# Second attention: values of eight heads per token block by three fp32r products of 512 columns from split latent rows and value weights

## The chip, the cores and the metric

The kernel runs on one core of one Trainium2 chip. The metric is the device time of one execution in microseconds (us), lower is better. The engines are named as in the profile: PE is TensorE, PEld its weight loads, DVE VectorE, ACT ScalarE, POOL GpSimd, SP SyncE, whose queue issues most of the loads.

## The reference

The program is two layers of a decoder trunk over 512 tokens of width 1024. Layer 0 mixes tokens by stick-breaking attention, layer 1 by a sparse attention over a latent of 128 values per token; each layer ends in a gated MLP with a short convolution. The change is in layer 1's attention, which is, cut to what matters:

```python
def dsa_attention(h, w_in, q_gain, k_gain, w_uv, w_out, rel_bias):
    q, lat, qi, ki, wi = jnp.split(h @ w_in, [o1, o2, o3, o4], axis=-1)
    q = rms_norm(q.reshape(B, S, 16, 128), q_gain)
    k = rms_norm(lat, k_gain)
    vals = lat
    def block(qb, t):                       # 128 queries at a time
        ...                                 # sel: the 128 keys picked by the indexer
        logits = jnp.einsum('bqhd,bqkd->bqhk', qb, k[bidx, sel]) * scale + bias
        p = jax.nn.softmax(jnp.where(valid, logits, NEG), axis=-1)
        return jnp.einsum('bqhk,bqkd->bqhd', p, vals[bidx, sel])
    o_lat = ...                             # (1, 512, 16, 128)
    o = jnp.einsum('bshl,hlv->bshv', o_lat, w_uv)   # w_uv: (16, 128, 64)
    return o.reshape(B, S, 1024) @ w_out
```

Inputs and results are float32. The kernel uses that the last two steps can be swapped: it first makes per-head values lat x w_uv[h] (512 tokens x 64) and then weights these.

## The kernel before

Tokens are in four blocks of 128. The attention of layer 1 loops over the 16 heads (index h in the code). While the weights of head h are transposed and used, the logits of head n = h + 1 are made. For each head n and each query block j, `logits(n, j)` is three fp32r products (high x high, low x high, high x low) into a PSUM bank z; `softmax(n, j)` is one custom instruction on DVE that adds the masked bias and takes the row maximum (line 1933); `expo(n, j)` is the exponential on ACT (line 2220). `transposed(h, i)` turns the weights of head h on PE in three groups i = 0, 1, 2 (line 2230), the first copied out by ACT (line 2235), the other two by DVE (line 2237). The bias of head h + 2 is prepared by ACT or POOL and masked by POOL (lines 2198, 2200, 2201).

Each engine works its queue in order, and the queue's order is the order in which the code issues the work. Between these steps `fill(n)` puts n steps of other work into PE's queue, three fp32r products each (lines 694 to 696): first the projections of the last q heads (pt_q), then the output projection (pt_o). `follow(engine)` issues what such a step leaves behind on ACT or DVE: the splitting of q (lines 1839, 1840, 1846), of weights (line 644 on ACT and 653 on POOL), and, after the last q head, the sums of squares of the last four q heads: `group_sum(3)`, four fp32 products "ssg" into the bank x (line 1863), copied out by ACT (line 1869).

PSUM has three banks mm, two z, two tr and one x. The bank x is used by the values "pv" and by ssg of the last q group.

Values are made for a pair of heads at a time. `pair_values(h)` is called in every odd iteration for the pair (h - 1, h), between the last logits of the next head and the third group of transposes (in the last iteration after the first group). It is four fp32 products, one for each block of 128 tokens: the latent `latf` is the stationary operand, 128 columns of the value weights `uvc` (two heads) move, and ACT copies the bank to SBUF. `weighted(h)` follows in the next iteration: for each block of keys and each of the two heads one fp32 product with 64 columns of values as the stationary operand (line 2261). Its output is scaled and split into the operands of the output projection (`pair_hi`, `pair_lo`: lines 2296, 2304, 2308).

A "split" of an fp32 tile is a copy on ACT that rounds to fp32r (the high part) and a subtraction on DVE (the low part). `LATE_STEPS` lists how many filler steps stand at each of the three places of an iteration.

Of the kernel before, what the change touches and what calls it, by code (L numbers as in the profile page):

```python
# [9 lines left out]
F32 = mybir.dt.float32  # L10
F32R = mybir.dt.float32r
BF = mybir.dt.bfloat16
AF = mybir.ActivationFunctionType
# [6 lines left out]
S = 512  # L20
P = 128
KT = D // P
QT = S // P
# [550 lines left out]
def kernel_body(ctx, tc, xT, wst, cst, smalls, crow, ccol, relb, outT):  # L574
    nc = tc.nc
    act, dve, pe, pool = nc.scalar, nc.vector, nc.tensor, nc.gpsimd
# [6 lines left out]
    npool = ctx.enter_context(tc.tile_pool(name="npool", bufs=1))  # L583
# [4 lines left out]
    def ptile(shape, name, tag):  # L588
        return banks.tile(shape, F32, name=name, tag=tag, bufs=nbanks[tag])
# [81 lines left out]
    def chunk(key, ahead=AHEAD):  # L671
        if ahead or key not in ready:
            prefetch(order.index(key) + ahead)
        return ready.pop(key)
# [1135 lines left out]
    def dsa_layer(l, first, man):  # L1810
        with ExitStack() as st:
            pp = st.enter_context(tc.tile_pool(name="dsa", bufs=1))
            hs = hcur["h"]
            latf = pp.tile([P, S], F32, name="latf")
# [13 lines left out]
            def project_steps(ps, ck):  # L1828
                whi, wlo = ck
                for k in range(KT):  # L1830
                    w = slice(k * P, (k + 1) * P)
                    mm3(ps, whi[:, w], wlo[:, w], hs[k][0], hs[k][1], k == 0, k == KT - 1)
                    yield
# [59 lines left out]
            def q_newton(h0, h1):  # L1893

                c = slice(h0 * QT, h1 * QT)
                dve.tensor_mul(irq[:, c], rq[:, c], rq[:, c])
                dve.scalar_tensor_tensor(irq[:, c], msq[:, c], EPS, irq[:, c], op0=OP.add, op1=OP.mult)
                dve.scalar_tensor_tensor(rq[:, c], irq[:, c], 3.0, rq[:, c], op0=OP.subtract, op1=OP.mult)
                dve.tensor_scalar(rq[:, c], rq[:, c], -0.5 * P ** -0.5, None, op0=OP.mult)
                dve.reciprocal(irq[:, c], rq[:, c])  # L1900
                act.activation(irq[:, c], irq[:, c], AF.Copy, scale=-1.0)
# [7 lines left out]
            def load_bias(h, th=None):  # L1909
                ths[h] = ap.tile([P, S], F32, name="th", bufs=2) if th is None else th  # L1910
                ov = relb[h:h + 1, 0:1]
                nc.sync.dma_start(ths[h], bass.AP(tensor=ov.tensor, offset=ov.offset, ap=[[1, P], [1, S]]))
# [25 lines left out]
            with ExitStack() as si:  # L1938
# [136 lines left out]
                for h in range(2, EARLY_Q):  # L2075
                    pt = ptile([P, S], "pt_q", "mm")
                    g = project_steps(pt, chunk(("dq", h), 0))
# [40 lines left out]
            with ExitStack() as sa:  # L2118
                ap = sa.enter_context(tc.tile_pool(name="att_d", bufs=2))
                O = []  # L2120
                uvc = [npool.tile([P, S], F32, name="uvc", tag="sqt", bufs=2) for i in range(2)]
# [43 lines left out]
                def fill(n):  # L2165
                    for _ in range(n):
                        next(filler, None)
# [41 lines left out]
                def logits(h, j):  # L2209
                    z = heads[h][3][j] = ptile([P, S], "z", "z")  # L2210
                    logits_into(z, h, j)
# [12 lines left out]
                def transposed(h, pi, by_act):  # L2224
                    tr = ptile([P, S], "tr", "tr")
                    w = TRW[pi]
                    for i, c0 in TRP[pi]:
                        for j in range(i, QT):
                            c = c0 + (j - i) * P
                            pe.transpose(tr[:, c:c + P], Ls[h, j][:, i * P:(i + 1) * P], ident)  # L2230
                    if pi == 0:
                        trs[h] = ap.tile([P, LW], F32, name="pT", bufs=2)
                    t = trs[h][:, TRO[pi]:TRO[pi] + w]
                    if by_act:
                        act.activation(t, tr[:, :w], AF.Copy)
                    else:
                        dve.tensor_copy(t, tr[:, :w])

                vals = {}

                def pair_values(h):

                    pv = ptile([P, S], "pv", "x")
                    for k in range(QT):
                        pe.matmul(pv[:, k * P:(k + 1) * P], lhsT=latf[:, k * P:(k + 1) * P],
                                  rhs=uvc[h // 8][:, h % 8 * 64:h % 8 * 64 + P], start=True, stop=True)
                    vals[h] = npool.tile([P, S], F32, name="vals", tag="u", bufs=3)
                    act.activation(vals[h], pv, AF.Copy)

                def weighted(h):  # L2250

                    av = pair["av"] = ptile([P, S], "av", "mm")
                    ts = [trs.pop(h + e) for e in range(2)]
                    vs = vals.pop(h)
                    for pi in range(3):
                        for i, c0 in TRP[pi]:
                            n = S - i * P
                            c = TRO[pi] + c0
                            for e in range(2):
                                hc = i * P + 64 * e  # L2260
                                pe.matmul(av[64 * e:64 * e + 64, i * P:], lhsT=vs[:, hc:hc + 64],
                                          rhs=ts[e][:, c:c + n], start=i == 0, stop=pi == 2)

                def pair_sums(rv):
# [61 lines left out]
                masked_bias(1, 3)  # L2326
                load_bias(3)
                rvb = None

                def sums(h):  # L2330

                    dve.reciprocal(heads[h][2][:, h % 2], heads[h][1])
                    if h % 2 and h < HEADS - 1:
                        pair_spread(heads[h][2])
                    return pair_sums(heads[h][2]) if h == HEADS - 1 else None

                for h in range(HEADS):
                    n = h + 1
                    more = n < HEADS
                    values = h % 2 == 0 and h > 0  # L2340
                    if more:
                        begin(n)
                        for j in range(2):
                            logits(n, j)
                        softmax(n, 0)
                        expo(n, 0)
                    if values:
                        weighted(h - 2)
                    fill(LATE_STEPS[h][0])
                    transposed(h, 0, True)  # L2350
                    if more:
                        softmax(n, 1)
                        expo(n, 1)
                        sums(h)
                    else:
                        rvb = sums(h)
                        pair_values(h - 1)
                    follow(dve)
                    if h == 3:
                        q_newton(8, EARLY_Q)  # L2360
                    if h == HEADS - 2:
                        late_dots(2)
                    if not more:
                        late_dots(1)
                    if h + 2 < HEADS:
                        masked_bias(h + 2, 0)
                    fill(LATE_STEPS[h][1])
                    if h == 10:
                        follow(dve, 1)
                    if more:  # L2370
                        logits(n, 2)
                        softmax(n, 2)
                        expo(n, 2)
                    transposed(h, 1, False)
                    if "row" in pair:
                        pair_rows()
                    if h + 2 < HEADS:
                        masked_bias(h + 2, 1)
                    if h == 10:
                        follow(dve)  # L2380
                    if more:
                        logits(n, 3)
                        softmax(n, 3)
                        expo(n, 3)
                    if h % 2 and more:
                        pair_values(h - 1)
                    transposed(h, 2, False)
                    if h + 2 < HEADS:
                        for j in range(2, QT):
                            masked_bias(h + 2, j)  # L2390
                    if n + 3 < HEADS:
                        load_bias(n + 3)
                    if h == 1:
                        q_seed(8, EARLY_Q)
                    if values:
                        pair_hi()
                    elif h > 1:
                        pair_lo()
                    fill(LATE_STEPS[h][2])
                    follow(act)  # L2400
                    if h == HEADS - 4:
                        load_dots(3)
                        bias_job(2, "col")
                    if h == 7:
                        follow(dve)
                    if not more:
                        pair_scale(rvb)
# [139 lines left out]
```

## Time and profile before

| | |
|---|---|
| median of 3 runs | 1213.65 us (1213.58 to 1214.35) |
| profiled execution | 1213.79 us, span of its instructions 1212.0 us |
| instructions | 18325 |
| products of the values (pv) | 64 records at line 2245, from 734.4 to 833.9 us |
| granted TensorE clock | 1.00 |

The timeline gives, for each instruction or run of equal ones, start and duration in us from the span's start, engine, line, operation, output<-inputs by the program's names, shape and count; in brackets stand the idle time of the engine before it and what ended it. Matmuls are pipelined: their durations overlap, so their pace is read from their starts. An fp32 product shows as two records. The table by stretches gives length, then busy time and count for PE, PEld, DVE, ACT and POOL, then the granted clock, the DMA share and GB/s.

### The profile page before, as it was taken

How to read it: one execution, taken by the hardware profiler on the slowest of the kernel's cores; microseconds unless marked ns; L12 is line 12 of the kernel's file. 1: busy time of each engine (PE TensorE's matmuls, PEld its weight loads, DVE VectorE, ACT ScalarE, POOL GpSimd, SP SyncE). 2: the span in 40 equal slices, each digit the busy share in tenths (PEclk: the TensorE clock that was granted, in tenths of full speed). 3: DMA queues.
4: the chain of work that ended last, by engine and by line, in shares of the span. 5: the costliest groups of instructions: out<-in, count | busy, mean ns of one | idle time of the engine just before them, and what ended most of it. 6: DMA issues, size and time to landing. Idle time of an engine off the chain costs nothing.

```text
span 1212.0 us, 18325 instructions
## 1 busy us (share of the span) xinstructions
PE 1205.1 (99%) x6532; PEld 1008.3 (83%) x6532; DVE 1032.0 (85%) x1800; ACT 799.8 (66%) x1366; POOL 242.8 (20%) x268
## 2 busy tenths in 40 slices
PE   9999999999999999999999999999999999999998
PEld 6878788788898998998888777777888888888887
DVE  5899888998989989999788995668989898889883
ACT  5588786478666676765657357774786677677660
POOL 0001100001111111211000457884012122112110
PEclk9999999999999999999999999999999999999999
DMA  9668887529889898897520252245499888788662
GB/s 376 236 193 228 231 248 241 202 82 229 192 209 276 230 251 226 221 288 169 189 71 18 71 139 55 88 135 169 132 235 215 224 191 204 183 182 191 153 149 87
DMA packets 79923, 224.50 MB, mean 185 GB/s; under 512 B 16588, under 2 KB 17356, under 8 KB 79832
## 3 DMA queue, kind: packets, MB, share of 16 engines
q1 hardware_dynamic: 59616, 168.77, 42.4%
q0 software_dynamic: 20192, 54.54, 25.3%
q8 instruction: 51, 0.84, 0.3%
q14 instruction: 40, 0.33, 0.1%
q10 hardware_dynamic: 24, 0.02, 0.0%
HBM read 212.23 MB, written 2.16 MB: 177 GB/s over the span
## 4 chain that ended last, share of the span: by engine, by line
PE 97%; DMA 1%; DVE 1%; ACT 1%; issue 0%; SPq 0%; DVEq 0%; ACTq 0%
PE pt_d L1737 16%; PE pt_a L1649 8%; PE pt_u L1618 6%; PE pt_a L1645 6%; PE pt_d L1649 4%; PE pt_u L1622 3%; PE pt_d L1645 3%; PE pt_q L694 2%; PE pt_l L694 2%; PE pt_q L696 2%; PE pt_l L696 2%; PE pt_q L695 2%; PE pt_l L695 2%; PE pt_b L1649 2%; PE pt_qk L694 2%; PE pt_fv L1099 2%
## 5 line engine op out<-in xcount | busy, mean ns | idle before, releaser
L1737 PE MATMUL pt_d<-actlo,dnhi 128*128 128x512 f32 x288 | 112.7, 391 | 0.0
L1737 PE MATMUL pt_d<-acthi,dnhi 128*128 128x512 f32 x288 | 112.7, 391 | 0.0
L1527 ACT ACTIVATE whi<-raw 128x1024 fp32r<-128x1024 f32 x72 | 75.8, 1054 | 29.1 <-PE pt_a L1649 13.2
L644 ACT ACTIVATE whi<-raw 128x1024 fp32r<-128x1024 f32 x80 | 84.2, 1052 | 3.8 <-issue 1.1
L1618 PE MATMUL pt_u<-hh,whi 128*128 128x512 f32 x320 | 75.8, 389 | 0.0
L1737 PE MATMUL pt_d<-acthi,dnlo 128*128 128x512 f32 x288 | 73.5, 390 | 0.0
L662 POOL DMA_DIRECT2D wlo<-wst x23 | 19.9, 866 | 267.3 <-DVE hh L806 115.1
L1618 PEld LDWEIGHTS pt_u<-hh,whi 128*128 128x128 f32 x320 | 60.0, 188 | 12.5
L1539 POOL DMA_DIRECT2D wlo<-wst x37 | 32.0, 865 | 168.5 <-ACT wlo L1535 69.8
L1737 PEld LDWEIGHTS pt_d<-actlo,dnhi 128*128 128x128 f32 x288 | 54.2, 188 | 10.2
L1737 PEld LDWEIGHTS pt_d<-acthi,dnhi 128*128 128x128 f32 x288 | 54.2, 188 | 10.1
L1737 PEld LDWEIGHTS pt_d<-acthi,dnlo 128*128 128x128 f32 x288 | 53.1, 188 | 10.3
L653 POOL TENSOR_TENSOR wlo<-raw,whi 128x1024 fp32r<-128x1024 f32 x18 | 44.2, 2457 | 85.6 <-PE pt_q L695 45.8
L1645 PE MATMUL pt_a<-hh,whi 128*128 128x512 f32 x228 | 61.3, 390 | 0.0
L722 DVE SCALAR_TENSOR_TENSOR raw<-raw,cond 128x1024 f32<-128x1024 f32 x46 | 57.3, 1273 | 1.4 <-ACT cond L1167 1.3
L1649 PE MATMUL pt_a<-hh,wlo 128*128 128x256 f32 x360 | 57.4, 282 | 0.0
L1649 PEld LDWEIGHTS pt_a<-hh,wlo 128*128 128x128 f32 x360 | 53.1, 190 | 4.5
L1346 DVE TENSOR_TENSOR_SCAN mz<-mz,diag 128x128 f32<-128x128 f32 (+1 forms) x64 | 52.5, 820 | 5.2 <-ACT mz L1341 4.9
L1933 DVE CUSTOM_DVE_ANT_0 L<-z,L,cols 128x128 f32<-128x128 f32 (+3 forms) x60 | 32.3, 546 | 28.8 <-PE tr L2230 20.7
L1550 POOL DMA_DIRECT2D whi<-wst x30 | 26.0, 866 | 133.0 <-ACT whi L1547 82.8
L694 PE MATMUL pt_q<-hh,whi 128*128 128x512 f32 x128 | 51.8, 405 | 0.0
L722 DVE SCALAR_TENSOR_TENSOR ada<-ada,cond 128x1024 f32<-128x1024 f32 x41 | 50.0, 1219 | 2.0 <-DMA ada<-wst 2.0
(408 smaller groups left out, 3806.8 us busy)
## 6 DMA issues: line engine op xcount, KB each, us to landing
raw<-wst SPq DMA_DIRECT2D x215, 512.0 KB, 5.1
wlo<-wst POOLq DMA_DIRECT2D x60, 512.0 KB, 8.0
ada<-wst SPq DMA_DIRECT2D x45, 512.0 KB, 5.5
raw<-wst SPq DMA_DIRECT2D x48, 384.0 KB, 4.9
whi<-wst POOLq DMA_DIRECT2D x30, 256.0 KB, 5.7
dnlo<-wst POOLq DMA_DIRECT2D x16, 384.0 KB, 7.0
x<-xt POOLq DMA_DIRECT2D x18, 256.0 KB, 5.3
th<-relb SPq DMA_DIRECT2D x16, 256.0 KB, 3.7
```

The source lines that it names most:

```text
L644: act.activation(hi[:, :n], raw[:, :n], AF.Copy)
L653: engine.tensor_sub(lo[:, :w], raw[:, :w], hi[:, :w].bitcast(F32))
L694: pe.matmul(out, lhsT=whi, rhs=ahi, start=start, stop=False)
L695: pe.matmul(out, lhsT=wlo, rhs=ahi, start=False, stop=False)
L696: pe.matmul(out, lhsT=whi, rhs=alo, start=False, stop=stop)
L722: dve.scalar_tensor_tensor(raw, raw, 1.0, cond, op0=OP.mult, op1=OP.mult, accum_out=dst)
L1346: dve.tensor_tensor_scan(rev, rev, diag[:, S - ns:][:, ::-1], 0.0, OP.mult, OP.max)
L1527: act.activation(W[j, i][0], R[j, i], AF.Copy)
L1618: pe.matmul(pt[j, i], lhsT=W[j, i][0][:, k * P:(k + 1) * P], rhs=hs[k][n], start=k + n == 0, stop=False)
L1645: pe.matmul(pt[j, bank, "both"], lhsT=w[:, c0 + k * P:c0 + (k + 1) * P], rhs=a[2], start=new and k == 0, stop=False, skip_group_check=True)
L1649: pe.matmul(out, lhsT=w[:, c0 + k * P:c0 + (k + 1) * P], rhs=a[n], start=new and k + n == 0, stop=part == 1 and k == 3 and what in ("a2", ...
L1737: pe.matmul(pt["dn", i], lhsT=dn[i][part][:, k * P:(k + 1) * P], rhs=A[j0 + k][n], start=part + k + n == 0, stop=part == 1 and k == j1 - j ...
```

## The change

The values are no longer made for two heads and all four blocks, but for eight heads (512 columns) and one block. The latent and the value weights are split into high and low fp32r parts, `lath`, `latl` and, for each group g of eight heads, `uvh`, `uvl`. One call of `group_values(g, k)` makes the values of block k for group g by three fp32r products of 512 columns into the bank x, which ACT copies out. The eight calls stand in four iterations, two for each group: `value_at` maps (head, place) to (group, block). The places are 0: after the first group of transposes, 1: after the second, 2: between the last logits and the third group. The latent and the weights of group 0 are split ahead of the loop, those of group 1 in iteration 6. `weighted` takes its 64 columns from `vals[h // 8, i]`. Of a group's four blocks three lie in the buffers "u", which held head 0's weights, and the fourth in that of its `uvc`.

```diff
-                def pair_values(h):
+                value_at = {(0, 2): (0, 0), (1, 0): (0, 1), (1, 1): (0, 2), (1, 2): (0, 3),
+                            (8, 0): (1, 0), (8, 2): (1, 1), (9, 0): (1, 2), (9, 2): (1, 3)}
+
+                def spread_values(h, at):
+                    if (h, at) in value_at:
+                        group_values(*value_at[h, at])
+
+                lath = ap.tile([P, S], F32R, name="lath", bufs=1)
+                parts = {"lat": (lath, npool.tile([P, S], F32R, name="latl", tag="ln"))}
+
+                def split_lat():
+                    act.activation(lath, latf, AF.Copy)
+                    dve.tensor_sub(parts["lat"][1], latf, lath.bitcast(F32))
+
+                def split_uv(g):
+                    parts[g] = [ap.tile([P, S], F32R, name="uv" + n, bufs=1) for n in "hl"]
+                    act.activation(parts[g][0], uvc[g], AF.Copy)
+                    dve.tensor_sub(parts[g][1], uvc[g], parts[g][0].bitcast(F32))
+
+                def group_values(g, k):
 
                     pv = ptile([P, S], "pv", "x")
-                    for k in range(QT):
-                        pe.matmul(pv[:, k * P:(k + 1) * P], lhsT=latf[:, k * P:(k + 1) * P],
-                                  rhs=uvc[h // 8][:, h % 8 * 64:h % 8 * 64 + P], start=True, stop=True)
-                    vals[h] = npool.tile([P, S], F32, name="vals", tag="u", bufs=3)
-                    act.activation(vals[h], pv, AF.Copy)
+                    (lh, ll), (uh, ul) = parts["lat"], parts[g]
+                    c = slice(k * P, (k + 1) * P)
+                    pe.matmul(pv, lhsT=lh[:, c], rhs=uh, start=True, stop=False)
+                    pe.matmul(pv, lhsT=lh[:, c], rhs=ul, start=False, stop=False)
+                    pe.matmul(pv, lhsT=ll[:, c], rhs=uh, start=False, stop=True)
+                    tag, bufs = ("u", 3) if k < 3 else ("sqt", 2)
+                    vals[g, k] = npool.tile([P, S], F32, name="vals", tag=tag, bufs=bufs)
+                    act.activation(vals[g, k], pv, AF.Copy)
...
+                split_lat()
+                split_uv(0)
...
                     transposed(h, 0, True)
+                    spread_values(h, 0)
...
-                        pair_values(h - 1)
                     follow(dve)
                     if h == 3:
                         q_newton(8, EARLY_Q)
+                    if h == 6:
+                        split_uv(1)
...
                     transposed(h, 1, False)
+                    spread_values(h, 1)
...
-                    if h % 2 and more:
-                        pair_values(h - 1)
+                    spread_values(h, 2)
                     transposed(h, 2, False)
```

Three places in the engines' queues matter. The first is DVE's queue at the start of head 1's logits (iteration 0). `L` are the masked biases, `th` the bias rows, "ISA" is the maximum of line 1933 and the read of its result; numbers behind a name tell buffers apart. Before:

```order
L1846 TENSOR_TENSOR ql<-pt_q,qh 128x512
L2196 TENSOR_SCALAR L_7379<-th_7230,cols 128x512
L1933 ISA L_7341,nm<-z,L_7341,cols 128x128
L1933 ISA nm 128x1
L1933 ISA L_7363,nm<-z,L_7363,cols 128x256
```

and now:

```order
L1846 TENSOR_TENSOR ql<-pt_q,qh 128x512
L2196 TENSOR_SCALAR L_7381<-th_7230,cols 128x512
L2252 TENSOR_TENSOR latl<-latf,lath 128x512
L2257 TENSOR_TENSOR uvl<-uvc,uvh 128x512
L1933 ISA L_7343,nm<-z,L_7343,cols 128x128
L1933 ISA nm 128x1
L1933 ISA L_7365,nm<-z,L_7365,cols 128x256
```

Two subtractions stand ahead of the first maximum of head 1. In the same way one subtraction stands in iteration 6 between the reciprocal and the maximum of head 7's third block (three of the rows around it):

```order
L2354 RECIPROCAL rv<-sum 128x4
L2257 TENSOR_TENSOR uvl<-uvc,uvh 128x512
L1933 ISA L_7907,nm<-z,L_7907,cols 128x384
L1933 ISA nm 128x1
L2237 COPY pT<-tr 128x512
```

It needs the high part, which ACT makes behind the exponential of head 7's second block. The third place is around the sums of squares of the last q group, at the end of iteration 8. ACT's queue before, from the last exponential of head 9 (`ohi` is the output's split, `whi` that of a weight):

```order
L2220 ACTIVATE L_8061,sum<-L_8061,nm 128x512
L2200 ACTIVATE L_8142<-th,cols 128x384
L2200 ACTIVATE L_8145<-th,cols 128x512
L2304 ACTIVATE ohi<-bo 128x512
L644 ACTIVATE whi<-raw 128x1024
L1869 ACTIVATE sums<-ssg 128x512
L2220 ACTIVATE L_8110,sum<-L_8110,nm 128x128
L2235 ACTIVATE pT<-tr 128x512
L2220 ACTIVATE L_8129,sum<-L_8129,nm 128x256
```

and now:

```order
L2220 ACTIVATE L_8069,sum<-L_8069,nm 128x512
L2269 ACTIVATE vals<-pv 128x512
L2200 ACTIVATE L_8162<-th,cols 128x384
L2200 ACTIVATE L_8165<-th,cols 128x512
L2324 ACTIVATE ohi<-bo 128x512
L644 ACTIVATE whi<-raw 128x1024
L1869 ACTIVATE sums<-ssg 128x512
L2220 ACTIVATE L_8124,sum<-L_8124,nm 128x128
L2235 ACTIVATE pT<-tr 128x512
L2269 ACTIVATE vals<-pv 128x512
```

The copy of ssg out of the bank x now stands between two copies of values out of the same bank. PE's queue at that place, now:

```order
L2264 MATMUL pv<-uvh,lath 128x512
L2265 MATMUL pv<-uvl,lath 128x512
L2266 MATMUL pv<-uvh,latl 128x512
L2230 MATMUL tr<-cons,L_7991 128x128
L2230 MATMUL tr<-cons,L_7994 128x128
L694 MATMUL pt_o<-ohi,whi 128x512
L695 MATMUL pt_o<-ohi,wlo 128x512
L696 MATMUL pt_o<-olo,whi 128x512
L1863 MATMUL ssg<-q2l,ones_r 32x512 x4
L1921 MATMUL z<-kph,qh 128x128
L1922 MATMUL z<-kph,ql 128x128
L1923 MATMUL z<-kpl,qh 128x128
```

Before, the three pv rows at its head were not there; after the rows shown come the second logits of head 10, the first transposes of head 9, and then, now, the values of block (9, 0), where before the filler products stood at once. In the prediction a group product is named by its (head, place).

More of the change, by code (lines that the diff above doesn't have):

```diff
@@ L2253, in weighted @@
                     ts = [trs.pop(h + e) for e in range(2)]
-                    vs = vals.pop(h)
                     for pi in range(3):
@@ L2259, in weighted @@
                             for e in range(2):
-                                hc = i * P + 64 * e
-                                pe.matmul(av[64 * e:64 * e + 64, i * P:], lhsT=vs[:, hc:hc + 64],
+                                hc = (h % 8 + e) * 64
+                                pe.matmul(av[64 * e:64 * e + 64, i * P:], lhsT=vals[h // 8, i][:, hc:hc + 64],
                                           rhs=ts[e][:, c:c + n], start=i == 0, stop=pi == 2)
```

## The prediction

> **What bounds the kernel now.** I read the busy shares first, then the chain that ended last, then one stage in the timeline: the second attention, from the first logits of head 1 to the first product after it.
>
> ```profile
> PE 1205.1 (99%) x6532; PEld 1008.3 (83%) x6532; DVE 1032.0 (85%) x1800; ACT 799.8 (66%) x1366; POOL 242.8 (20%) x268
> ...
> PE 97%; DMA 1%; DVE 1%; ACT 1%; issue 0%; SPq 0%; DVEq 0%; ACTq 0%
> ```
> ```profile
> 724.06:842.00 117.94, 116.75 (x724) 92.37 (x723) 80.67 (x218) 83.03 (x207) 86.20 (x95) 1.00 0.38 109
> ```
>
> TensorE (PE) is busy for 99% of the span and carries 97% of the chain. In this stage it is busy for 116.75 of 117.94 us at a granted clock of 1.00, while the vector engine (DVE) has 80.67 us of work and the scalar engine (ACT) 83.03. So a product taken from TensorE is time won, and a wait put into TensorE's queue is time lost: nothing behind it can pass. What follows is a count of both.
>
> **The products.** Below, z(n,j) are the logits of head n, query block j; tr(h,i) the i-th group of transposes of head h.
>
> ```profile
> 734.12 0.39 PE L1923 MATMUL z<-kpl,qh 128*128 128x512 f32 x1
> 734.35 1.05 PE L2245 MATMUL pv<-uvc,latf 128*128 128x128 f32 x8
> 735.24 0.27 PE L2230 MATMUL tr<-cons,L 128*128 128x128 f32 x1
> ...
> 743.24 0.40 PE L1923 MATMUL z<-kpl,qh 128*128 128x512 f32 x1
> 743.48 0.38 PE L2230 MATMUL tr<-cons,L 128*128 128x128 f32 x2
> ```
> ```profile
> L2245 PE MATMUL pv<-uvc,latf x64: 270/275/275, 734.4 to 833.9; 128*128 128x128 f32 x64
> ```
>
> Durations of matmuls overlap, so starts are read. A pair's four fp32 products (eight records, 64 in all for eight pairs) hold TensorE from 734.35 to 735.24, 0.89 us; in the even head at 743.24 the transposes follow the logits after 0.24 at once. Removed: 8 x 0.89 = 7.12 us. An fp32r product of 512 columns takes 0.23, start to start (734.12 to 734.35). Added: 8 groups of three, 24 x 0.23 = 5.52. Net: 1.60 us less. No more changes between fp32 and fp32r arise than before, since the new products stand beside logits, fillers and transposes as the old did. The evacuations stay eight of the same shape on ACT.
>
> **A gain that doesn't all arrive: head 3.** Six of the eight pairs now find their values ready long before; only weighted(0) and weighted(8) still follow a group closely. One wait for values is in the trace:
>
> ```profile
> 751.36 0.74 DVE L1933 CUSTOM_DVE_ANT_0 L<-z,L,cols 128x512 f32<-128x512 f32 x1
> 752.16 0.38 PE L1921 MATMUL z<-kph,qh 128*128 128x256 f32 x1
> 752.50 0.28 PE L1923 MATMUL z<-kpl,qh 128*128 128x256 f32 x1
> 753.49 0.65 PE L2261 MATMUL av<-pT,vals 128*64 128x512 f32 x2 [0.71 <-ACT vals L2248]
> ```
>
> The wait of 0.71 goes, and 0.89 of product ahead of it too. But z(5,1) at 752.16 starts 0.06 after DVE's maximum of z(4,3) ends (751.36 + 0.74 = 752.10): with TensorE earlier, that maximum is what is late next, and DVE's queue there doesn't depend on the product removed. The weighted product then starts 0.21 after 752.50 at the earliest (0.28 less overlap), 752.71 instead of 753.49. So 0.78 is won at this pair, not 0.89: +0.11 against the sum above. The other odd heads I take at the full 0.89.
>
> **The splits at head 0.** ACT gets two copies and DVE two subtractions ahead of the first maximum of head 1. Their operands are there: latf since the indexer, uvc loaded during the last q projections.
>
> ```profile
> 725.11 0.19 ACT L2220 ACTIVATION_READ_ACCUMULATOR Lu<-Lu,cols 128x1 f32 x1
> 725.30 0.77 DVE L2196 TENSOR_SCALAR L<-th,cols 128x512 f32<-128x512 f32 x1
> 725.99 0.34 DVE L1933 CUSTOM_DVE_ANT_0 L<-z,L,cols 128x128 f32<-128x128 f32 x1
> 726.15 1.16 POOL L2201 TENSOR_TENSOR L<-L,maskb 128x512 f32<-128x512 f32 x1 [0.36 <-DVE L L2196]
> 726.91 0.33 PE L1921 MATMUL z<-kph,qh 128*128 128x384 f32 x1
> ```
> ```profile
> 788.85 0.62 ACT L2304 ACTIVATE ohi<-bo 128x512 fp32r<-128x512 f32 x1
> ```
> ```profile
> 778.56 0.93 POOL L2198 TENSOR_SCALAR L<-th,cols 128x256 f32<-128x256 f32 x1
> 779.10 0.68 DVE L2308 TENSOR_TENSOR olo<-bo,ohi 128x512 fp32r<-128x512 f32 x1
> ...
> 825.24 1.47 DVE L722 SCALAR_TENSOR_TENSOR raw<-raw,cond 128x1024 f32<-128x1024 f32 x1
> 825.58 3.39 POOL L653 TENSOR_TENSOR wlo<-raw,whi 128x1024 fp32r<-128x1024 f32 x1
> 826.64 3.40 DVE L722 SCALAR_TENSOR_TENSOR raw<-raw,cond 128x1024 f32<-128x1024 f32 x1
> ```
>
> The nearest rows to a split are those of the attention's output: 0.62 on ACT, 0.68 on DVE. ACT is free at 725.21 to 725.30, so lath is there by 725.92 and DVE can start latl at 726.00. GpSimd (POOL) has its mask addition L2201 ready at 726.15. At 825.24 such a case stands in the trace: DVE starts, POOL starts 0.34 later and takes 3.39, and DVE's next instruction, of the same kind, then takes 3.40 and ends after POOL: the two take turns whole. I read head 0 the same way: latl 726.00 to 726.68, POOL to 727.84, uvl to 728.52, and only then the maximum of z(1,0), 2.53 late. z(1,2) wants that bank, so it starts at 728.52 + 0.34 + 0.06 = 728.92, not 726.91: TensorE waits 2.01. Bounds: without turns both subtractions are done at 726.00 + 2 x 0.68 = 727.36, and 727.36 + 0.40 - 726.91 = 0.85; if POOL also goes first with its next instruction (0.61, the row at 772.67 below), 2.6. Against the turns speaks the row at 779.10: 0.68 beside a POOL instruction. I keep them, because POOL's instruction here (L2201, a tensor_tensor) is of the kind at 825.58, not of that at 778.56.
>
> The Trainium skill (SBUF — State Buffer, Who interferes with whom) says that a DVE instruction with two SBUF inputs contends with a GpSimd instruction that reads SBUF, and that whichever issues first holds the shared port for the whole instruction. The pair at 825.58 and 826.64 agrees, the pair at 778.56 and 779.10 does not show it; by the rule the sum is my forecast, without it that of the second rival.
>
> **Head 1.** The only bank for values (x) must be emptied between one block and the next, and its evacuation stands behind an exponential on ACT.
>
> ```profile
> 733.53 0.62 DVE L1933 CUSTOM_DVE_ANT_0 L<-z,L,cols 128x384 f32<-128x384 f32 x1 [0.23 <-PE tr L2230]
> 734.19 0.62 ACT L2220 ACTIVATE L<-L,nm 128x384 f32<-128x384 f32 x1 [0.26 <-DVE nm L1933]
> 734.71 0.19 ACT L2220 ACTIVATION_READ_ACCUMULATOR L<-L,nm 128x1 f32 x1
> ...
> 779.27 0.58 ACT L2248 ACTIVATE vals<-pv 128x512 f32<-128x512 f32 x1
> ```
>
> Beside head 0's wait, which moves all engines alike, z(2,2) and with it this chain is two groups later (1.38): the row at 734.71 comes at 736.09, the values of (1,1) are emptied from 736.19 to 736.77. TensorE, three groups later (2.07), wants (1,2) at 734.35 + 2.07 = 736.42 and gets the bank at 736.83: a wait of 0.41. Weighted(0) stands behind two filler steps and the first logits of head 3, so its values are in time.
>
> **The split at head 6.** uvh follows the second exponential on ACT; uvl stands on DVE ahead of the maximum of z(7,2).
>
> ```profile
> 770.30 2.40 POOL L653 TENSOR_TENSOR wlo<-raw,whi 128x1024 fp32r<-128x1024 f32 x1
> 771.67 0.19 ACT L2220 ACTIVATION_READ_ACCUMULATOR L<-L,nm 128x1 f32 x1
> 772.11 0.62 DVE L1933 CUSTOM_DVE_ANT_0 L<-z,L,cols 128x384 f32<-128x384 f32 x1 [3.59 <-PE tr L2230]
> 772.67 0.61 POOL L2198 TENSOR_SCALAR L<-th,cols 128x128 f32<-128x128 f32 x1
> 774.04 0.72 ACT L2220 ACTIVATE L<-L,nm 128x512 f32<-128x512 f32 x1 [0.56 <-DVE nm L1933]
> 774.55 0.49 PE L2230 MATMUL tr<-cons,L 128*128 128x128 f32 x3
> ```
>
> DVE idles for 3.59 us before this maximum, but uvh is finished only at 771.77 + 0.62 = 772.39, so that idle time can't be used. POOL holds until 772.70, uvl runs to 773.38, and the maximum is 1.27 late. So is the exponential at 774.04, which ends (774.76) just as TensorE's fourth transpose of head 7 wants it: no slack, 1.27 of wait. Bounds: 1.02 without turns; 1.9 if POOL's next instruction (772.67, 0.61) goes first.
>
> **Heads 8 and 9.** The sums of squares of the last four q heads (ssg) use the same bank x, between blocks (8,2) and (9,0).
>
> ```profile
> 786.92 1.07 PE L1863 MATMUL ssg<-q2l,ones_r 128*32 128x512 f32 x8
> 787.01 0.72 ACT L2220 ACTIVATE L<-L,nm 128x512 f32<-128x512 f32 x1 [0.56 <-DVE nm L1933]
> 787.73 1.21 ACT L2200 ACTIVATE L<-th,cols 128x384 f32<-128x384 f32 x2
> ...
> 789.06 0.48 PE L694 MATMUL pt_o<-ohi,whi 128*128 128x512 f32 x1
> 789.37 1.04 ACT L644 ACTIVATE whi<-raw 128x1024 fp32r<-128x1024 f32 x1
> 790.32 0.57 ACT L1869 ACTIVATE sums<-ssg 128x512 f32<-128x512 f32 x1
> ```
>
> Block (8,0) makes everything 0.69 later; on ACT the evacuation of (8,2) starts where L2200 did, 787.73 + 0.69 = 788.42, and ends at 789.00. TensorE, two groups later, reaches ssg at 788.30 and waits to 789.06: 0.76. On ACT, L2200 twice, ohi, L644 and the evacuation of ssg take 790.32 + 0.57 - 787.73 = 3.16, so x is free at 792.16. TensorE wants (9,0) where pt_o stood, 789.06 + 1.38 + 0.76 = 791.20, and gets the bank at 792.22: 1.02.
>
> **The sum.** -1.60 + 0.11 + 2.01 + 0.41 + 1.27 + 0.76 + 1.02 = +3.98 us. The profiled execution took 1213.79 us around a span of 1212.0; its own new time would be 1217.8. The median of the runs is 0.14 lower, 1213.65, so the forecast is 1217.6. TensorE carries the chain to the end, so the delay goes through. No DMA is added or moved on any queue.
>
> **Rivals.**
> - The bank is free in time. ACT is idle for 30% of the stage; if its queue ran ahead at heads 1, 8 and 9, 0.41 + 0.76 + 1.02 = 2.19 falls away: 1215.4, not slower by what can be told (0.2%, 2.4 us, is about what a measurement tells from no change). It decides once more than 1.6 of the 2.19 is hidden. Against it: from 787.01 to 790.89 ACT's rows follow each other without a gap.
> - DVE and POOL don't take turns: 2.01 becomes 0.85 and 1.27 becomes 1.02, 1.41 less: 1216.2.
> - POOL goes first twice: 0.6 more at each split: 1218.8.
> - Only the products count, the waits hide: -1.5, 1212.2. For it speaks that DVE and ACT have a third of the stage free; against it, that each place above is in-order and named.
>
> **Numbers.** Forecast 0.52 (own range 1216.6 to 1218.6), bank in time 0.12, no turns 0.18, POOL twice 0.08, products alone 0.10. Slower: the forecast, the fourth case and 0.11 of the third, 0.71. Faster: 0.06, the part of the last case in which the wait for values at head 3 and others like it are won in full too. Same: the rest, 0.23. The range 1214.6 to 1219.6 reaches from the first two rivals together with a little slack to POOL twice and late values at weighted(0) or weighted(8).
>
> **What would show it.** In the trace after: pv as 24 rows at 0.23 steps; z of block 2 of head 1 waiting some 2 us for DVE; ssg and the next pv waiting for ACT 0.8 and 1.0; a late fourth transpose at head 7; uvl longer than 0.68. If those waits are missing, I am wrong towards 1212; if pv steps at more than 0.23, towards more.

## The result, and the profile after

The changed kernel takes 1220.69 us (median of 6 runs, 1220.47 to 1221.36), the kernel before 1213.64 (6 runs beside them): 1.0056 times as long, interval 1.0046 to 1.0067. The forecast was 1217.6, its range ended at 1219.6. Slower was right; of 7.05 us the sum held 3.98.

The page of the changed kernel, its busy times and its chain, then the table by stretches for the same stage, from the first logits of head 1 to the first product after the attention:

```profile
PE 1206.5 (99%) x6492; PEld 1006.3 (83%) x6492; DVE 1036.2 (85%) x1803; ACT 801.0 (66%) x1369; POOL 243.8 (20%) x268
...
PE 88%; DVE 6%; ACT 3%; DMA 1%; issue 1%; POOL 0%; SPq 0%; DVEq 0%; ACTq 0%
```
```profile
724.06:849.00 124.94, 118.37 (x685) 89.63 (x684) 85.05 (x222) 84.71 (x210) 87.40 (x95) 1.00 0.36 103
```

The stage is 7.00 us longer (124.94 for 117.94), which is the whole difference. TensorE is idle in it for 6.57 us instead of 1.19, and the chain runs through DVE for 6% of the span instead of 1%. TensorE's waits in this stage (what waits, for what; us in total, times, longest):

```profile
PE z L1921 <- DVE nm L1933: 3.3, 4, 1.5
PE av L2281 <- DVE pT L2237: 1.1, 1, 1.1
PE ssg L1863 <- ACT vals L2269: 0.7, 1, 0.7
PE pv L2264 <- ACT sums L1869: 0.7, 1, 0.7
PE tr L2230 <- DVE pT L2237: 0.3, 1, 0.3
PE pv L2264 <- ACT vals L2269: 0.2, 1, 0.2
PE tr L2230 <- ACT pT L2235: 0.2, 1, 0.2
```

The first, third, fourth and sixth row are waits of the sum. The second, fifth and seventh are not in it. To size them I laid TensorE's starts in both profiled executions side by side and read by how much each instruction is later than before. This difference is -0.06 just ahead of the first wait, +4.50 at the first filler product behind the first transposes of head 15 (833.96 before, 838.46 now), and +6.80 at the last of head 15's weighted products (838.61 before, 845.41 now). So the loop up to that filler costs 4.56, where the sum had 3.98, and the last few microseconds cost 2.30, where the sum had nothing.

These are the rows of that end, before, in order of time on all engines:

```profile
834.24 0.60 ACT L2248 ACTIVATE vals<-pv 128x512 f32<-128x512 f32 x1
834.74 1.05 ACT L644 ACTIVATE whi<-raw 128x1024 fp32r<-128x1024 f32 x1
...
835.83 0.17 DVE L726 TENSOR_TENSOR mod<-mod,sm 128x8 f32<-128x8 f32 x1
835.87 2.38 POOL L653 TENSOR_TENSOR wlo<-raw,whi 128x1024 fp32r<-128x1024 f32 x1 [6.90 <-ACT whi L644]
835.92 1.01 DVE L2237 COPY pT<-tr 128x512 f32<-128x512 f32 x2
...
836.61 2.37 PE L2261 MATMUL av<-pT,vals 128*64 128x512 f32 x16
```

And now:

```profile
839.84 1.05 ACT L644 ACTIVATE whi<-raw 128x1024 fp32r<-128x1024 f32 x1
840.97 2.63 POOL L653 TENSOR_TENSOR wlo<-raw,whi 128x1024 fp32r<-128x1024 f32 x1 [6.40 <-ACT whi L644]
841.43 2.19 DVE L726 TENSOR_TENSOR mod<-mod,sm 128x8 f32<-128x8 f32 x1
841.49 1.72 PE L2281 MATMUL av<-pT,vals 128*64 128x512 f32 x6
843.55 1.01 DVE L2237 COPY pT<-tr 128x512 f32<-128x512 f32 x2
844.28 1.51 PE L2281 MATMUL av<-pT,vals 128*64 128x384 f32 x10 [1.07 <-DVE pT L2237]
```

Line 726 adds 8 columns; it took 0.17 before. Before, it started 0.04 ahead of GpSimd's subtraction of line 653; now it starts 0.46 behind it and takes 2.19, until GpSimd is done (840.97 + 2.63 = 843.60). The copies of the transposed weights stand behind it in DVE's queue, and the weighted products wait for them. GpSimd starts when ACT's line 644 has made `whi`; before, the evacuation of the last pair's values stood ahead of line 644 on ACT, and the change has taken it away there.

Three theories follow, one for each part of the 7 us. T1: the end of the loop costs about 1.9 because GpSimd now goes ahead of line 726. T2: bank x with one user behind the other costs about 1.7 at heads 8 and 9 (0.75 and 0.91). T3: the subtractions of the splits in DVE's queue cost 1.65 at head 0 and 1.27 at head 6. The expectations below have 1.68 and 1.26 for T3, and 1.03 for the second wait of T2, which there includes that the first product behind the wait lasts longer. Against each theory stands that something else is late there anyway.

### The profile page after: what moved, and what is told of

The parts are those of the page before. It is cut to its first block, busy times and chain, and to the rows that moved or that the text cites. A ratio compares the mean times of both kernels' runs of the same rounds, so it can differ in the third digit from the quotient of the medians.

```text
span 1219.0 us, 18252 instructions
## 1 busy us (share of the span) xinstructions
PE 1206.5 (99%) x6492; PEld 1006.3 (83%) x6492; DVE 1036.2 (85%) x1803; ACT 801.0 (66%) x1369; POOL 243.8 (20%) x268
## 4 chain that ended last, share of the span: by engine, by line
PE 88%; DVE 6%; ACT 3%; DMA 1%; issue 1%; POOL 0%; SPq 0%; DVEq 0%; ACTq 0%
PE pt_d L1737 16%; PE pt_a L1649 8%; PE pt_u L1618 6%; PE pt_a L1645 6%; PE pt_d L1649 4%; PE pt_u L1622 3%; PE pt_d L1645 3%; PE pt_l L694 2%; PE pt_l L696 2%; PE pt_l L695 2%; PE pt_b L1649 2%; PE pt_fv L1099 2%; PE pt_first L694 2%; PE pt_first L695 2%; PE pt_first L696 2%; DVE work L2005 2%
## 5 line engine op out<-in xcount | busy, mean ns | idle before, releaser
L2201 POOL TENSOR_TENSOR L<-L,maskb 128x128 f32<-128x128 f32 (+3 forms) x60 | 47.5, 803 | 23.1 <-ACT L L2200 19.6
```

Of the source, the lines that this page charges most:

```text
L2201: pool.tensor_add(L, L, maskb[:, LOFF[j]:LOFF[j] + ns])
```

## The experiments

In each comparison the kernel before ran on the same chip (median 1213.62 for the first four, 1213.67 for the last four). Differences below are against the 1220.69 of the changed kernel unless another is named. That one was not run again beside them, and the ratios to before have intervals of about 0.1% (1.2 us) to either side, so the smallest differences (1.25 and 1.00 in experiments 2 and 3) rest on two things: none of their runs (at most 1219.92 and 1220.05) reaches the changed kernel's fastest (1220.47), and the traces show where the time went.

**1. Line 726 behind the copies.**

```diff
+                held_sum = []
...
                         if f == KT - 1:
-                            ada_sum(l, g)
+                            held_sum.append(g)
...
                     transposed(h, 2, False)
+                    while held_sum:
+                        ada_sum(l, held_sum.pop())
```

> Only in iteration 15: the small addition of line 726 (128x8, two SBUF inputs) stands behind the copies of the transposed weights in DVE's queue instead of ahead of them. Theory T1 (the end of the attention loses its time because GpSimd's subtraction of line 653 now starts ahead of this addition, which then waits for it and holds the copies): the copies go through beside the subtraction, the wait of 1.07 before the weighted products of the last pair goes, 843.80 - 841.49 - 0.39 = 1.92 us less: 1218.8. Rival (the copies were late because of their transposes or of ACT): no change, 1220.7.

1218.96 us (ratio to before 1.0042, 1.003 to 1.0055), 1.73 less. The rows of the end, with line numbers two higher:

```profile
841.29 2.65 POOL L653 TENSOR_TENSOR wlo<-raw,whi 128x1024 fp32r<-128x1024 f32 x1 [6.41 <-ACT whi L644]
841.64 1.02 DVE L2239 COPY pT<-tr 128x512 f32<-128x512 f32 x2
841.82 2.37 PE L2283 MATMUL av<-pT,vals 128*64 128x512 f32 x16
842.57 1.39 DVE L726 TENSOR_TENSOR mod<-mod,sm 128x8 f32<-128x8 f32 x1
```

GpSimd still starts first. The copies, whose input lies in PSUM, run beside it in 1.02 (1.01 in the kernel before); the addition, with two inputs in SBUF, again lasts until GpSimd is done (841.29 + 2.65 = 843.94), but nobody waits for it. The weighted products are one run of 16 again. Against the changed kernel's, this execution was 0.33 late at the first of them (841.82 for 841.49) and 1.59 early at the last (843.82 for 845.41): 1.92, as T1 has it. So T1's size and place hold; in the medians one 128x8 instruction in the wrong place of a queue was worth 1.7 us.

**2. Work added on ACT instead.**

```diff
                         rvb = sums(h)
+                        for _ in range(2):
+                            act.activation(lath, latf, AF.Copy)
```

> Only in iteration 15: two copies of the latent (128x512) are put back on ACT ahead of line 644, into a tile that nobody reads any more; they stand for the evacuation that stood there before the change. Work is added, none taken away. T1: line 644 ends about 1.05 us later, GpSimd's subtraction starts at about 842.0 instead of 840.97, behind the addition of line 726 (841.43), which takes 0.17 again: 1.9 us less, 1218.8, though work was added. Rival (ACT or the transposes were late): no change or up to 1 us more, 1220.7 to 1221.7.

1219.44 us (1.0048, 1.0035 to 1.006), 1.25 less, by two useless copies. DVE's and GpSimd's rows:

```profile
841.84 0.17 DVE L726 TENSOR_TENSOR mod<-mod,sm 128x8 f32<-128x8 f32 x1
842.55 2.37 POOL L653 TENSOR_TENSOR wlo<-raw,whi 128x1024 fp32r<-128x1024 f32 x1 [7.59 <-ACT whi L644]
842.86 2.61 DVE L2328 TENSOR_TENSOR olo<-bo,ohi 128x512 fp32r<-128x512 f32 x1
```

The addition takes 0.17 again, and the weighted products end 1.50 earlier in the trace; since this execution was 0.42 late at the first of them, that is 1.92 here too. The wait isn't gone, though: it has moved on to the subtraction `olo` behind the copies, which lasts 2.61 and holds up the next instruction on DVE (`bs`, at 845.39, where experiment 1 has it at 844.49). Some 0.6 of the 1.50 is given back later, in small steps from 881 us on. Whether the late `olo` and `bs` cause them was not tried: this execution (1219.92) is the slowest of the five, and a step of 0.4 that no edit explains stands at 982 us in experiment 4, too.

**3. Bank x for the sums of squares alone.**

```diff
-                            (8, 0): (1, 0), (8, 2): (1, 1), (9, 0): (1, 2), (9, 2): (1, 3)}
+                            (8, 0): (1, 0), (8, 1): (1, 1), (9, 1): (1, 2), (9, 2): (1, 3)}
```

> The four products of group 1 move: from places (8,0), (8,2), (9,0), (9,2) to (8,0), (8,1), (9,1), (9,2), so that the sums of squares have bank x for themselves between them. T2 (one bank, three users in a row: 0.75 at ssg and 1.03 at block (9,0)): both waits go, 1.78 less, and a new one of up to 0.4 between (9,1) and (9,2), which follow each other closely: 1.4 to 1.8 less, 1218.9 to 1219.3. Rival (TensorE waits there for logits or weights that are late anyway, and the bank only ends last): under 0.5 less, 1220.2 or more.

1219.69 us (1.0049, 1.0035 to 1.0063), 1.00 less: outside T2's 1.4 to 1.8, on its side of the rival's 0.5. Laid beside the changed kernel, TensorE is 0.75 earlier from ssg on and 0.94 more where block (9,0) had waited, so both waits go, as T2 has it. But the new wait came as well, at (9,2):

```profile
797.81 0.50 PE L2264 MATMUL pv<-uvh,lath 128*128 128x512 f32 x1 [0.32 <-ACT vals L2269]
```

It costs 0.48 by starts and 0.59 with the first product behind it, where T2 had allowed 0.4. Of the miss of 0.3 in the trace, 0.2 is this, and 0.1 is that the wait at block (9,0) was worth 0.94 and not 1.03. So the bank is the cause of both waits, and two blocks with one group of logits between them are too close for it.

**4. No subtractions.**

```diff
-                    dve.tensor_sub(parts["lat"][1], latf, lath.bitcast(F32))
+                    parts["lat"] = (lath, lath)
...
-                    dve.tensor_sub(parts[g][1], uvc[g], parts[g][0].bitcast(F32))
+                    parts[g] = [parts[g][0]] * 2
```

> The three subtractions on DVE (latl, uvl of both groups) are left out, and the high parts stand in for the low ones in the products, so their number and shape stay. T3 (the waits at heads 0 and 6 come from these subtractions in DVE's queue and from taking turns with GpSimd): 1.68 and 1.26 go, 2.94 less, 1217.8. Rival a (ACT's copies are what holds DVE and the exponentials up): 0 to 0.5 less. Rival b (turns alone): as T3, but the waits left would be those of unhindered subtractions, which aren't there either; so T3 and b aren't told apart here, only in the trace by the durations of the subtractions with the change (0.68, 1.64).

1217.32 us (1.0032, 1.0019 to 1.0044), 3.37 less. TensorE's starts are 1.65 earlier at head 0 and 1.27 at head 6, together 2.92, which is the whole of both waits. Where the other 0.4 comes from isn't shown: the profiled execution (1218.76) is the slowest of the five. ACT's copies stayed, so rival a falls.

**5. The trap in the kernel before.** The kernel before with its last evacuation of values behind line 644 on ACT, nothing else moved:

```diff
                     vals[h] = npool.tile([P, S], F32, name="vals", tag="u", bufs=3)
-                    act.activation(vals[h], pv, AF.Copy)
+                    if h < HEADS - 2:
+                        act.activation(vals[h], pv, AF.Copy)
+                    return pv
...
-                        pair_values(h - 1)
+                        last_pv = pair_values(h - 1)
...
                     if not more:
+                        act.activation(vals[h - 1], last_pv, AF.Copy)
                         pair_scale(rvb)
```

> The kernel before, with one move in iteration 15: ACT's evacuation of the last pair's values stands behind line 644 instead of ahead of it. The products stay where they were, nothing is added. T1: GpSimd's subtraction of line 653 starts at about 835.37 instead of 835.87, ahead of the addition of line 726 (835.83), which then lasts until about 838.0; the copies of the transposed weights end 838.9, the second part of the last weighted products starts at 838.73 and ends 1.25 later than before: 1214.9. Rival (the end of the loop was slow only because of what else the change did): no change, 1213.6.

1214.86 us (11 runs, 1214.6 to 1215.61; ratio 1.001, 1.0001 to 1.0019), 1.19 more than 1213.67, where T1 gave 1.25:

```profile
835.17 2.65 POOL L653 TENSOR_TENSOR wlo<-raw,whi 128x1024 fp32r<-128x1024 f32 x1 [6.41 <-ACT whi L644]
835.64 2.21 DVE L726 TENSOR_TENSOR mod<-mod,sm 128x8 f32<-128x8 f32 x1
837.77 1.01 DVE L2237 COPY pT<-tr 128x512 f32<-128x512 f32 x2
838.50 1.51 PE L2263 MATMUL av<-pT,vals 128*64 128x384 f32 x10 [0.37 <-DVE pT L2237]
```

The old kernel shows the same picture once GpSimd starts 0.47 ahead of line 726. No product, split or bank of the change is needed for it, so T1 stands as a cause of its own.

**6. The subtractions elsewhere.** `split_lat` and `split_uv` keep ACT's copies alone; `lat_lo` and `uv_lo` are their subtractions on DVE, issued where the diff shows.

```diff
+                    if h == 2:
+                        split_uv(1)
...
-                    if h == 6:
-                        split_uv(1)
+                    if h == 0:
+                        lat_lo()
+                        uv_lo(0)
+                    if h == 2:
+                        uv_lo(1)
```

> The changed kernel with its three subtractions at other places in DVE's queue: latl and uvl of group 0 behind head 0's reciprocal, that is behind the first two maxima of head 1 instead of ahead of them; group 1's split in iteration 2 (its ACT part behind the first exponential of head 3, its DVE part behind the reciprocal). All work stays. T3: of head 0's 1.68 some 1.3 goes, of head 6's 1.26 all, 2.6 less: 1218.1. Rival (a subtraction costs its time wherever it stands, since DVE is what is late): at most 0.5 less, 1220.2.

1217.81 us (1.0034, 1.0021 to 1.0046), 2.88 less. All the work is still there:

```profile
726.77 1.10 DVE L2254 TENSOR_TENSOR latl<-latf,lath 128x512 fp32r<-128x512 f32 x1
726.93 0.33 PE L1921 MATMUL z<-kph,qh 128*128 128x384 f32 x1
727.31 1.56 POOL L2198 TENSOR_SCALAR L<-th,cols 128x128 f32<-128x128 f32 x1
727.80 0.68 DVE L2261 TENSOR_TENSOR uvl<-uvc,uvh 128x512 fp32r<-128x512 f32 x1
```

The third logits of head 1 start at 726.93, as in the kernel before (726.91): the subtraction still waits for GpSimd (1.10), but nothing urgent stands behind it. By TensorE's starts 1.65 goes at head 0, all of its cost and more than the 1.3 expected, and 1.0 at head 6, where 1.26 was expected. It is the place in the queue that cost the time, so the rival falls.

**7 and 8. All mends at once.** Line 726 as in 1, the subtractions as in 6, and

```diff
-                            (8, 0): (1, 0), (8, 2): (1, 1), (9, 0): (1, 2), (9, 2): (1, 3)}
+                            (7, 2): (1, 3), (8, 0): (1, 0), (8, 1): (1, 1), (9, 1): (1, 2)}
...
+                    if h == 11:
+                        fill(1)
                     transposed(h, 2, False)
```

with `LATE_STEPS[11]` (0, 2, 0) instead of (0, 2, 1); in the second of the two, moreover, `pool.tensor_sub` for the three `dve.tensor_sub`.

> All mends at once: the subtractions moved as in the run before, line 726 behind the copies as in the first experiment, the sums of squares with bank x to themselves (group 1 at (7,2), (8,0), (8,1), (9,1)), and at head 11 one filler step ahead of the third group of transposes instead of behind it, as a cover for the wait of 0.30 there. If the terms are independent: 1220.7 - 1.92 - 1.78 - 2.6 - 0.4 = 1214.0, level with the kernel before (0.4 above). If the causes hang together (each wait taken away shows another behind it): 1215.5 or more. If only the products' 1.60 were left: 1212.1.

> As the run before, but the three subtractions are done by GpSimd instead of DVE. Terms as there, without the remainder at head 0 (0.4): 1213.6, if GpSimd's mask additions behind them are still in time. Rival: GpSimd's subtractions hold the shared port, and DVE's instructions with two SBUF inputs (and through them the logits of head 1) wait for them as at head 0 before: 1 to 2 us more, 1215 to 1216.

With DVE: 1213.86 us (11 runs, 1213.51 to 1214.54; ratio 1.0002, 0.9993 to 1.0011), level with before. With GpSimd: 1214.67 (1.0008, 0.9999 to 1.0017), between the two expectations and for another reason than the rival's: GpSimd needs 1.30 and 1.26 for its first two subtractions and the second comes too late for the product itself. A row of this kernel, and then all of TensorE's waits in the stage for the one with DVE:

```profile
729.79 0.50 PE L2271 MATMUL pv<-uvl,lath 128*128 128x512 f32 x1 [0.89 <-POOL uvl L2263]
```
```profile
PE z L1921 <- DVE nm L1933: 1.1, 2, 0.7
PE tr L2232 <- ACT pT L2237: 0.2, 1, 0.2
```

The sum of the terms holds: 1214.0 expected, 1213.86 measured. The 1.60 of the products isn't left over as time: by TensorE's starts waits remain at heads 1 (0.5), 3, 5 and 9 (0.1 each), 6 (0.4) and 15 (0.6). Even a version without any of them would end at about 1212.1, 0.13% below before, no more than the half width of most intervals here (0.09 to 0.14%). So no version that beats the kernel before was found.

## Why the prediction was right or wrong

Term by term, the forecast and what TensorE's starts in the profiled execution show:

| term | forecast | shown |
|---|---|---|
| group of three products | 0.69 | 0.70 at each of the five that can be read singly |
| product of a pair removed (heads 3, 5, 7, 11, 13, 15) | 0.89 | 0.89, 0.89, 0.90, 0.43, 0.89, 0.84 |
| head 3, remainder | 0.11 | 0.10 |
| splits at head 0 | 2.01 | 1.65, and 1.77 with the next product |
| bank x at head 1 | 0.41 | 0.39 |
| split at head 6 | 1.27 | 1.27, and 1.35 with the products behind it |
| bank x at ssg, at (9,0) | 0.76, 1.02 | 0.75, 0.91 |
| end of head 15 | none | 2.30 |

At three of the five groups the product behind starts 0.78 later and the one after it 0.70: the first fp32r product behind the fp32 transposes takes 0.31 to the next start instead of 0.23, before (731.23) as now (733.63), and it is now a product of the group. So the products were priced right.

**The splits: right in mechanism, one size off.** Rows of head 0, after:

```profile
725.94 0.68 DVE L2252 TENSOR_TENSOR latl<-latf,lath 128x512 fp32r<-128x512 f32 x1
726.10 1.54 POOL L2201 TENSOR_TENSOR L<-L,maskb 128x512 f32<-128x512 f32 x1 [0.36 <-DVE L L2196]
726.54 1.64 DVE L2257 TENSOR_TENSOR uvl<-uvc,uvh 128x512 fp32r<-128x512 f32 x1
727.62 1.04 POOL L2198 TENSOR_SCALAR L<-th,cols 128x128 f32<-128x128 f32 x1
728.11 0.34 DVE L1933 CUSTOM_DVE_ANT_0 L<-z,L,cols 128x128 f32<-128x128 f32 x1
...
728.51 0.44 PE L1921 MATMUL z<-kph,qh 128*128 128x384 f32 x1 [1.49 <-DVE nm L1933]
```

DVE, GpSimd and DVE take turns in the order of the forecast. I had added whole durations (0.68 + 1.16 + 0.68 from 726.00, end at 728.52); in the rows the turns overlap at their edges and uvl ends at 728.18, 0.34 earlier. At head 6 DVE's subtraction started at 774.96 and took 1.13, since GpSimd's line 653 ran until 775.54; that term's size held. Its place didn't: the sum had the wait at the fourth transpose of head 7, behind a late exponential, and this transpose falls back by no more than 0.03. TensorE waits earlier in its queue, ahead of the logits z(8,0) and z(8,1), for DVE's late maxima:

```profile
777.15 0.73 DVE L1933 CUSTOM_DVE_ANT_0 L<-z,L,cols 128x512 f32<-128x512 f32 x1
777.95 0.39 PE L1921 MATMUL z<-kph,qh 128*128 128x256 f32 x1 [0.72 <-DVE nm L1933]
```

The same maxima are the cause, so the right size was partly luck. The rival without turns (0.85 and 1.02) is refuted by the 1.64, and the rival in which GpSimd goes first twice by its order here.

**The bank: right.** ACT's evacuations and the instructions that waited for them:

```profile
791.45 0.58 ACT L2269 ACTIVATE vals<-pv 128x512 f32<-128x512 f32 x1
792.08 1.07 PE L1863 MATMUL ssg<-q2l,ones_r 128*32 128x512 f32 x8 [0.68 <-ACT vals L2269]
794.52 0.57 ACT L1869 ACTIVATE sums<-ssg 128x512 f32<-128x512 f32 x1
795.14 0.50 PE L2264 MATMUL pv<-uvh,lath 128*128 128x512 f32 x1 [0.67 <-ACT sums L1869]
```

The brackets count idle time behind modelled ends; by starts the waits are 0.75 and 0.91. The rival of a bank that is free in time falls with them and with experiment 3.

**The step that failed first: "The other odd heads I take at the full 0.89".** I had looked for what is late next at head 3 alone. At head 11 the next thing is the third group of transposes, before (first two rows) and now:

```profile
806.38 1.05 PE L2245 MATMUL pv<-uvc,latf 128*128 128x128 f32 x8
807.27 0.38 PE L2230 MATMUL tr<-cons,L 128*128 128x128 f32 x2
...
812.53 0.69 DVE L2237 COPY pT<-tr 128x512 f32<-128x512 f32 x1
813.27 0.44 PE L2230 MATMUL tr<-cons,L 128*128 128x128 f32 x2 [0.30 <-DVE pT L2237]
```

The removed product stood between the two groups and covered the copy that empties a bank for it; without it, 0.46 is lost. At head 15 the wait for ACT's copy looks the same (0.33), but no experiment takes it away. Put back as a cover, a filler step ahead of these transposes won some 0.5 at head 11 in the trace of experiment 7. This is most of the 0.6 by which the loop missed. The rest is small and nearly cancels: about 0.1 more each at block (1,2), head 5 and head 6, and 0.14 at head 15's first transposes, which now wait for an exponential, against 0.24 less at head 0 and some 0.2 less at heads 8 and 9.

**The step that failed most: head 15 had no term at all.** There the pair's product stands in another place, its evacuation another in ACT's queue, and the sum said "each place above is in-order and named", which was true of the places that gained an instruction and not of those that lost one. The mechanism was in the prediction, for head 0: whoever starts first holds the turn. The rows that would have given the price stood in the trace before: line 726 at 835.83 and GpSimd at 835.87, 0.04 apart. Of the 2.30, 0.38 is the wait for ACT's copy just named, with the transposition behind it, and 1.92 the held copies; experiments 1 and 2 take away 1.92 there in their traces (1.73 and 1.25 in the medians), experiment 5 makes 1.19 out of it in the kernel before, where DVE had reached line 726 earlier against TensorE.

The Trainium skill (SBUF — State Buffer, Who interferes with whom) says that a DVE instruction with two SBUF inputs contends with a GpSimd instruction that reads SBUF, and that the order of issue decides who blocks, not the shape. The 128x8 addition that takes 2.19 behind and 0.17 ahead of the same subtraction agrees, and so do the copies out of PSUM that run beside it at 1.02. A GpSimd tensor_scalar, which reads SBUF too, agrees only in part: it held DVE off only in the first part of its time, as the last section shows.

## What to carry to other kernels

Where instructions are taken out of an in-order queue, price the places that they leave: what stood behind them now starts earlier, and what they covered shows. If DVE and GpSimd both read two SBUF operands there, look for the pair whose starts lie closest, since a change elsewhere of half a microsecond can turn a 0.17 us instruction into one of over 2. Put such instructions behind what others wait for, not ahead of it.

## What the runs showed of the hardware

The turns aren't the same for all kinds of GpSimd instructions. A GpSimd tensor_tensor that started first held DVE's addition until it ended (2.19 for 0.17). GpSimd's tensor_scalar with one SBUF tensor (line 2198, 0.93 for 128x256) held DVE off only near its start:

```profile
782.45 0.93 POOL L2198 TENSOR_SCALAR L<-th,cols 128x256 f32<-128x256 f32 x1
782.65 0.82 DVE L2328 TENSOR_TENSOR olo<-bo,ohi 128x512 fp32r<-128x512 f32 x1
```

Here, after the change, DVE's subtraction starts 0.20 behind the tensor_scalar and takes 0.82 instead of its plain 0.68. At 0.26 behind it takes 0.76 (796.64 in experiment 7, with the subtractions on DVE), at 0.33 behind 0.69 (780.13 there), and at 0.54 behind 0.68 (779.10 in the kernel before). The distance and the delay add up to 0.34 in the first three (0.20 + 0.14, 0.26 + 0.08, 0.33 + 0.01), so as an estimate DVE is let through about 0.34 after the tensor_scalar's start. So the row at 779.10, which the prediction held against the turns, shows a late start and not an instruction that never holds DVE off.

The other way round the tensor_scalar waits: for 128x128 it takes 1.04 at 727.62 after the change and 1.56 at 727.31 in experiment 6, where it meets DVE's subtractions, against 0.61 at 772.67 before. In experiment 6 DVE's second subtraction (0.68 at 727.80) even went ahead of the tensor_scalar that had waited since 727.31.
